# A hybrid decoder layer on one core: the scratch for dynamic transfers goes from 2048 to 4096 bytes, and a 1 KB buffer moves into the 4 KB slots

## The chip, the cores and the metric

The kernel runs on one core of one Trainium2 chip. The metric is device time in microseconds of one execution. Three runs of the kernel before took 745.06, 747.29 and 750.37 us; the median is 747.29 us. A separate execution was profiled; it took 746.93 us, and the profiler saw a span of 745.2 us from its first to its last instruction.

## The reference

One decoder layer over 512 tokens of width 1024, in float32, cut to what matters here:

```python
xn = rms_norm(h, norm_mix)
proj = xn @ w_in                                  # 1024 x 3128
y_r = rwkv7_group(proj[..., :R_COLS], ...)        # 8 heads of 64, a recurrence over the tokens
y_n = nsa_group(proj[..., R_COLS:], ...)          # compressed, selected and window attention
h = h + concat([y_r, y_n]) @ w_out
h = h + (silu(n @ w_gate) * (n @ w_up)) @ w_down  # n = rms_norm(h, norm_ffn); d_ff = 2816
return rms_norm(h, norm_final)
```

In the attention group, keys and values are compressed: windows of 32 tokens, 16 apart, go through a two-layer MLP (`wk1`, `wk2` for the keys, `wv1`, `wv2` for the values) to 31 compressed tokens for each of the two key heads.

## The kernel before

**Arithmetic.** Each float32 operand of a large product is split into a rounded part and a rest (`split`, lines 149 and 151: ACT writes the rounded part, DVE subtracts it for the rest). A product is then three matmuls (`mm3`, lines 168 to 170).

**Stages, by the profiled span.** The input projection is cut into 16 jobs of some 256 columns (to about 205 us). With the jobs are woven the compressed keys (`hidden`, `compressed`) and the triangular solve of the recurrence (`solve`, `solve2`, `solve4`). The recurrence and the attention follow, woven together, to about 380 us; then the output projection and the second norm (to about 412 us), the feed-forward part (to about 600 us), and the down projection (to the end).

**The feed-forward part** is what most of the dynamic transfers belong to. The gate and the up matrix are cut into 11 column blocks, q = 0 to 10, of 256 columns (class `Weights`). Each block is multiplied with seven products in place of eight, in the manner of Strassen and Winograd, for which sums of weight quarters are needed: t1 = gate upper + up upper, t2 = t1 + up lower, t3 = up upper + up lower. A quarter is 512 x 256 floats, 512 KB; it lies in SBUF as 128 partitions by four rows of 1 KB. For all blocks but q = 1 two of the sums are made by transfers: SP loads a quarter plainly (lines 1173 and 1175), and then POOL issues an accumulating transfer of another quarter on top of it (lines 1177 for t1 and 1178 for t3). The lower up quarter (called b22, line 1174) is a plain load by SP. DVE then adds t1 and b22 (line 1184), and the sums are split into operands (lines 1185 to 1195). The even q hold t1, t2 and t3 in three `t4` slots, the odd q in one `L` slot. That is 20 accumulating transfers of 512 KB in 1 KB rows. The down projection has four more (line 1348), of 512 KB each in 2 KB rows.

**The scratch.** For the transfers that POOL issues the program reserves a scratch at the start of every partition of SBUF. Its size is the argument `dynamic_dma_scratch_size` of the program (line 1424). The tiles are laid out behind it.

**Slots.** Tiles with one tag share a fixed number of slots of the largest tile's size: `t4` has four slots of 4 KB, `rp` one of 1 KB, `L` four of 16 KB, `wraw` three of 8 KB. A tile waits for a slot until an older tile of the tag was last read.

**Order.** The kernel is written as one sequence. A planner (`schedule_with_timeline_sim=True`) orders each engine's instructions and hands out slots by going through the sequence with simulated times; `high_priority`, `rank` and `issue_after` in the code push parts of it forward or back. Each engine then runs its list strictly in order: an instruction that waits holds up all behind it on that engine. On DVE, for instance, line 1184 of one block stands ahead of the last splits of the operands that the block before still needs. POOL's list has the transfers as block 4's t3, block 6's t1, block 5's t1, block 5's t3, block 6's t3.

**The compressed keys.** `compressed` (lines 695 to 728) writes three small tiles with the tag `rp`: two copies `rp` (1 KB a partition, one for each key head, line 707) which the PE reads at line 709, and `kc2` (line 714). In the one slot each waits for the last read of the one before. At that time the `t4` slots hold `cm` (the weights and hidden values of the compression, last read at line 709), and then `blk` and `inv` of the solve and `qt2` of the recurrence.

Of the kernel before, what the change touches and what calls it, by code (L numbers as in the profile page):

```python
# [9 lines left out]
F32R = mybir.dt.float32r  # L10
# [36 lines left out]
def hybrid_layer(ctx: ExitStack, tc: tile.TileContext, x, positions, norm_mix, w_in, mu_shift, w0, w2, a0, a2,  # L47
                 g2, k_k, k_a, r_k, lnx_w, lnx_b, pe_k, wk1, bk1, wk2, pe_v, wv1, bv1, wv2, w_out, norm_ffn,
                 w_gate, w_up, w_down, norm_final, out):
    nc = tc.nc  # L50
# [11 lines left out]
    def ps(tag, shape=(128, 512), dtype=F32):  # L62
        return pp.tile(list(shape), dtype, name="ps_" + tag, tag=tag, bufs=PS_BUFS[tag])
# [4 lines left out]
    def st(shape, tag, bufs=1, dtype=F32):  # L68
        return sb.tile(list(shape), dtype, name=tag, tag=tag, bufs=SB_BUFS.get(tag, bufs))
# [168 lines left out]
    def rotate(o, src, tab, scale=1.0):  # L238

        with rank(200):  # L240
            m, tt, n = src.shape[0:3]
            ACT.activation(o, src, AF.Copy, scale=scale)
            ta, tb = (st([128, 8, 16], "rot", 2)[0:m, 0:tt * n].rearrange("p (t n) d -> p t n d", t=tt) for _ in range(2))
            cosv, sinv = (v[:, :, None, :].to_broadcast([m, tt, n, 16]) for v in tab)
            DVE.tensor_mul(ta, o[:, :, :, 0:16], cosv)
            for a in (0, 8):
                DVE.tensor_mul(tb[:, :, :, a:a + 8], o[:, :, :, 8 - a:16 - a], sinv[:, :, :, a:a + 8])
            DVE.tensor_add(o[:, :, :, 0:16], ta, tb)
# [445 lines left out]
    def compressed():  # L694

        p = ps("s")
        for u in range(2):
            PE.matmul(p[0:64, 0:64], hidT[:, 0, u], wc2[:, 0, u], start=u == 0, stop=u == 1)
        kct = st([64, 1, 1, 64], "kct")
        rotate(kct, p[0:64, None, None, 0:64], (rope[0:64, 0, 4:5], rope[0:64, 1, 4:5]))  # L700
        kct = kct[:, 0]
        vcb = st([128, 2, 4, 64], "lora")
        POOL.memset(vcb, 0.0)
        for g in range(2):
            p = ps("s")
            rp = st([128, 2, 4, 32], "rp")
            ACT.activation(rp, hidT[:, 1, :, None, g * 32:g * 32 + 32].to_broadcast([128, 2, 4, 32]), AF.Copy)
            for u in range(2):
                PE.matmul(p[:, 0:64], rp[:, u].rearrange("p a n -> p (a n)"), wc2[:, 1, u], start=u == 0, stop=u == 1)
            for h in range(4):  # L710
                DVE.tensor_copy(vcb[h * 32:h * 32 + 32, g, h], p[h * 32:h * 32 + 32, 0:64])
        kcA = st([128, 2, 2, 32], "kcA", dtype=F32R)
        kc2 = st([64, 4, 64], "rp", dtype=F32R)
        for a in range(2):
            ACT.activation(kc2[:, a], kct[:, 0], AF.Copy)
        for a in range(2):
            DVE.tensor_sub(kc2[:, 2 + a], kct[:, 0], kc2[:, 0].bitcast(F32))
        p = ps("s")
        for a in range(2):
            PE.transpose(p[:, a * 64:a * 64 + 64].bitcast(F32R), kc2[:, 2 * a:2 * a + 2].rearrange("p a d -> p (a d)"), identr[0:64, 0:64])  # L720
        kcA0 = st([128, 64], "rot", 2)
        POOL.memset(kcA0, 0.0)
        ACT.activation(kcA[:, :, 0], p[:, 0:64].rearrange("p (g n) -> p g n", g=2), AF.Copy)
        DVE.tensor_copy(kcA[:, :, 1], kcA0.rearrange("p (g n) -> p g n", g=2))
        for g in range(2):
            gs = slice(g * 64, g * 64 + 64)
            ACT.activation(kcA[gs, g, 1], p[gs, 64 + g * 32:96 + g * 32], AF.Copy)
        T.update(vcb=vcb, kcA=kcA)
# [24 lines left out]

    hk, hv = lambda: hidden(0, "bk1"), lambda: hidden(1, "bv1")
    jobs = [(None, job_lat), (load_tail, job_tail), (cols(1024), job_v(0)), mk[0], then((cols(1280), job_v(1)), gate), mk[1], then((cols(512), job_k(0)), hk), mv[0], (cols(768), job_k(1)), then(mv[1], hv), then((cols(0), job_r(0)), solve, compressed), (cols(256), job_r(1)), then((lambda: load_kv(128), job_vt), solve2), (lambda: load_kv(0), job_ks), then((cols(RCOLS), job_qs(0)), solve3, solve4), (cols(RCOLS + 256), job_qs(1))]

    moving = [jobs[i][1] for i in (3, 5, 7, 9, 12, 13, 14, 15)]
# [677 lines left out]
```

## Time and profile before

| | |
|---|---|
| median of three runs | 747.29 us (745.06 to 750.37) |
| the profiled execution | 746.93 us, span 745.2 us, so 1.73 us outside the span |
| PE busy | 720.3 us, 97% of the span |
| DVE, ACT, POOL busy | 591.9, 402.0, 150.8 us |
| mean granted TensorE clock | 0.983 |
| transfers issued by SP (plain) | 71.91 MB |
| transfers issued by POOL (accumulating) | 12.58 MB |

Busy time is by engine. Matmuls are pipelined and overlap in the records, so a busy PE can still be fed more slowly than it could run; the number of matmuls that start in a stretch tells more. A wait shown as "issue" is time in which the engine waited for nothing that the profile shows. A wait for several things is put down to the one that ended last by the records.

### The profile page before, as it was taken

What the parts mean: (1) busy time and instruction counts of PE and PEld (TensorE: products, weight loads), DVE (VectorE), ACT (ScalarE), POOL (GpSimd) and SP (SyncE); (2) the same over time, 40 slices, a digit from 0 to 9 for tenths busy, and PEclk for the clock granted to TensorE, in tenths of its full rate; (3) what the DMA queues carried; (4) which work ended last, traced back from release to release, by engine and by line L of the source; (5) the groups of instructions that cost most, each with busy time, mean ns of one, the idle gap of its engine ahead of it and who ended that gap; (6) DMA issues with size and microseconds to landing.
All of it is one profiled execution on the core that took longest, in us unless ns stands there. A gap on an engine that the chain in (4) does not pass through costs nothing.

```text
span 745.2 us, 14931 instructions
## 1 busy us (share of the span) xinstructions
PE 720.3 (97%) x6045; PEld 627.3 (84%) x6045; DVE 591.9 (79%) x1097; ACT 402.0 (54%) x670; POOL 150.8 (20%) x250
## 2 busy tenths in 40 slices
PE   6999999998989999999999999989999999999996
PEld 6967887898878788777788999989999999777885
DVE  4488778889767998888368999769796899999835
ACT  6388835325267865778438644444453455465414
POOL 3210030228434552354000001211110101000000
PEclk8999999999899999999999999999999999999998
DMA  7623543100044000140320668787868619352402
GB/s 254 200 88 113 168 115 113 58 2 1 2 144 114 3 2 2 34 138 1 111 88 1 157 188 221 185 181 173 213 166 215 143 63 324 122 118 109 142 0 113
DMA packets 71882, 85.44 MB, mean 115 GB/s; under 512 B 4948, under 2 KB 61350, under 8 KB 71814
## 3 DMA queue, kind: packets, MB, share of 16 engines
q1 hardware_dynamic: 60166, 71.91, 29.4%
q0 software_dynamic: 11648, 12.58, 10.9%
q8 instruction: 47, 0.77, 0.4%
q14 instruction: 21, 0.17, 0.1%
HBM read 82.39 MB, written 2.10 MB: 113 GB/s over the span
## 4 chain that ended last, share of the span: by engine, by line
PE 60%; DVE 22%; DMA 7%; issue 5%; ACT 4%; POOL 1%; SPq 0%; DVEq 0%; POOLq 0%; ACTq 0%
PE ps_ra L169 5%; PE ps_ra L170 5%; PE ps_ra L168 5%; PE ps_pj L170 5%; PE ps_pj L168 5%; PE ps_pj L169 5%; DVE wlo L151 4%; PE ps_o L1019 3%; DVE whi L151 3%; PE ps_pj L1010 2%; DVE L L151 2%; DMA L<-in_w_up_dram 2%; PE ps_s L170 2%; PE ps_s L168 2%; PE ps_s L169 2%
## 5 line engine op out<-in xcount | busy, mean ns | idle before, releaser
L149 ACT ACTIVATE whi<-wraw 128x1024 fp32r<-128x1024 f32 (+1 forms) x63 | 62.6, 1030 | 38.9 <-PE ps_ra L170 13.9
L151 DVE TENSOR_TENSOR wlo<-wraw,whi 128x1024 fp32r<-128x1024 f32 (+1 forms) x46 | 55.2, 1227 | 19.2 <-ACT whi L149 14.3
L1007 POOL TENSOR_SCALAR whi<-whi,m,gates 128x128 f32<-128x128 f32 (+3 forms) x64 | 46.3, 758 | 49.5 <-DVE m L1004 40.1
L170 PE MATMUL ps_ra<-L,wlo 128*128 128x512 f32 (+2 forms) x136 | 47.8, 352 | 0.0
L168 PE MATMUL ps_pj<-L,whi 128*128 128x512 f32 (+1 forms) x128 | 44.3, 351 | 0.5 <-DVE t L1261 0.4
L169 PE MATMUL ps_pj<-L,whi 128*128 128x512 f32 (+1 forms) x128 | 44.7, 349 | 0.0
L169 PE MATMUL ps_ra<-L,whi 128*128 128x512 f32 (+2 forms) x128 | 44.1, 344 | 0.0
L168 PE MATMUL ps_ra<-L,whi 128*128 128x512 f32 (+2 forms) x128 | 43.8, 344 | 0.0
L170 PE MATMUL ps_pj<-L,wlo 128*128 128x512 f32 (+1 forms) x128 | 43.2, 337 | 0.1
L1003 ACT ACTIVATE whi<-whi,m 128x128 f32<-128x128 f32 (+3 forms) x64 | 35.5, 556 | 7.2 <-DVE m L1002 6.8
L168 PE MATMUL ps_ra<-whi,L 128*128 128x256 f32 (+1 forms) x108 | 35.3, 330 | 0.5 <-ACT L L149 0.5
L169 PE MATMUL ps_ra<-wlo,L 128*128 128x256 f32 (+1 forms) x108 | 34.8, 323 | 0.2 <-DVE wlo L151 0.2
L170 PE MATMUL ps_pj<-whi,L 128*128 128x256 f32 (+1 forms) x108 | 34.9, 323 | 0.0
L169 PE MATMUL ps_pj<-wlo,L 128*128 128x256 f32 (+1 forms) x108 | 34.8, 322 | 0.0
L168 PE MATMUL ps_pj<-whi,L 128*128 128x256 f32 (+1 forms) x108 | 34.8, 325 | 0.0
L170 PE MATMUL ps_ra<-whi,L 128*128 128x256 f32 (+1 forms) x108 | 34.5, 322 | 0.0
L1002 DVE CUSTOM_DVE_ANT_0 whi<-ps_s,negb 128x128 f32<-128x128 f32 (+3 forms) x64 | 29.4, 484 | 3.0 <-PE ps_pj L1010 2.0
L170 PEld LDWEIGHTS ps_ra<-L,wlo 128*128 128x128 f32 (+1 forms) x136 | 25.1, 184 | 4.1 <-issue 0.5
L168 PEld LDWEIGHTS ps_pj<-L,whi 128*128 128x128 f32 x128 | 24.0, 188 | 4.3 <-DVE t L1261 0.8
L170 PE MATMUL ps_s<-L,whi 128*128 128x256 f32 (+1 forms) x88 | 26.2, 299 | 1.3 <-DVE whi L151 1.3
L1177 POOL DMA_DIRECT2D t<-in_w_up_dram x6 | 8.0, 1331 | 94.8 <-DVE b L1103 58.5
L170 PEld LDWEIGHTS ps_pj<-L,wlo 128*128 128x128 f32 x128 | 24.0, 188 | 3.5 <-DVE wlo L151 0.9
(708 smaller groups left out, 2546.7 us busy)
## 6 DMA issues: line engine op xcount, KB each, us to landing
wraw<-in_w_gate_dram SPq DMA_DIRECT2D x22, 512.0 KB
wraw<-in_w_in_dram SPq DMA_DIRECT2D x9, 1024.0 KB
wraw<-in_w_down_dram SPq DMA_DIRECT2D x9, 1024.0 KB
t<-in_w_up_dram POOLq DMA_DIRECT2D x12, 512.0 KB, 6.1
wraw<-in_w_up_dram SPq DMA_DIRECT2D x11, 512.0 KB
wraw<-in_w_out_dram SPq DMA_DIRECT2D x4, 1024.0 KB
L<-in_w_up_dram POOLq DMA_DIRECT2D x8, 512.0 KB, 6.8
wraw<-in_w_in_dram SPq DMA_DIRECT2D x6, 512.0 KB
```

Source lines behind the costliest of these rows:

```text
L149: ACT.activation(hi, src, AF.Copy)
L151: (POOL if pool else DVE).tensor_sub(lo, src, hi.bitcast(F32))
L168: PE.matmul(o, lh, rh, start=start, stop=False)
L169: PE.matmul(o, lh, rl, start=False, stop=False)
L170: PE.matmul(o, ll, rh, start=False, stop=stop)
L1002: DVE.tensor_tensor_reduce(pr[:, i], pS[:, i], negb[:, S - n:S], scale=-1.0, scalar=3e38, op0=OP.add, op1=OP.min, accum_out=m[:, i, 0:1])
L1003: ACT.activation(pr[:, i], pr[:, i], AF.Exp, scale=-1.0, bias=m[:, i, 0:1], accum_out=m[:, i, 1:2])
L1007: POOL.tensor_scalar(pr[:, i], pr[:, i], m[:, i, 2:3], gv[:, 1 + b0 + i, h:h + 1], op0=OP.mult, op1=OP.mult)
L1010: PE.transpose(pT[:, j], prr[:, x, j * 128:j * 128 + 128], ident)
L1019: PE.matmul(po[q, 2 * g:2 * g + 2], vtok[:, j % (t + 1), b0 + j // (t + 1), g], pTs[:, par, j], start=False, stop=g == 1 and bs[-1] == 1 a ...
L1177: POOL.dma_start(self.t1, self.quarter(w_up, 0), accum_op=OP.add)
```

## The change

The scratch gets twice its size. It takes 2048 bytes more of each partition. The three tiles of `compressed` get the tag `t4` in place of `rp`: the 1 KB slot of `rp` goes, and the tiles use the 4 KB slots that other tiles share. Nothing else in the source is changed; the planner goes through the changed program anew.

```diff
         for g in range(2):
             p = ps("s")
-            rp = st([128, 2, 4, 32], "rp")
+            rp = st([128, 2, 4, 32], "t4")
             ACT.activation(rp, hidT[:, 1, :, None, ...
...
-        kc2 = st([64, 4, 64], "rp", dtype=F32R)
+        kc2 = st([64, 4, 64], "t4", dtype=F32R)
...
-    nc = _bacc.Bacc("TRN2", ..., num_devices=1, dynamic_dma_scratch_size=2048)
+    nc = _bacc.Bacc("TRN2", ..., num_devices=1, dynamic_dma_scratch_size=4096)
```

## Rows read from the trace of the kernel before

**Rows 1.** The page, part 1: busy us (share of span) x instructions.

```profile
PE 720.3 (97%) x6045; PEld 627.3 (84%) x6045; DVE 591.9 (79%) x1097; ACT 402.0 (54%) x670; POOL 150.8 (20%) x250
```

**Rows 2.** PE's waits, 412 to 600 us: us in total, times, longest.

```profile
PE ps_pj L170 <- DVE wlo L151: 2.4, 1, 2.4
PE ps_ra L170 <- DVE wlo L151: 0.9, 1, 0.9
```

**Rows 3.** DVE's timeline: start, us, line, tiles, [idle before <-releaser].

```profile
497.85 1.23 DVE L1184 TENSOR_TENSOR L<-L,wraw 128x1024 f32<-128x1024 f32 x1 [6.97 <-DMA L<-in_w_up_dram]
499.59 1.22 DVE L151 TENSOR_TENSOR wlo<-wraw,wlo 128x1024 fp32r<-128x1024 f32 x1
...
536.64 1.23 DVE L1184 TENSOR_TENSOR L<-L,wraw 128x1024 f32<-128x1024 f32 x1 [3.77 <-DMA wraw<-in_w_up_dram]
...
577.77 1.23 DVE L1184 TENSOR_TENSOR L<-L,wraw 128x1024 f32<-128x1024 f32 x1 [5.84 <-DMA L<-in_w_up_dram]
```

**Rows 4.** Windows of 5 us: busy us (x starts) by engine, PEclk, DMA share, GB/s.

```profile
490.00:495.00 5.00, 5.00 (x45) 5.00 (x44) 0.88 (x1) 1.06 (x1) 1.30 (x1) 1.00 0.70 206
495.00:500.00 5.00, 3.50 (x31) 3.29 (x29) 2.15 (x3) 0.29 (x1) 1.29 (x1) 1.00 0.56 90
500.00:505.00 5.00, 4.14 (x23) 4.14 (x24) 5.00 (x7) 3.18 (x4) 0.77 (x1) 0.68 1.07 229
```

**Rows 5.** POOL's timeline, 475 to 493 us, columns as in rows 3.

```profile
475.34 1.29 POOL L1178 DMA_DIRECT2D t<-in_w_up_dram  x1 [7.99 <-issue]
481.62 1.29 POOL L1177 DMA_DIRECT2D t<-in_w_up_dram  x1 [4.99 <-DVE whi L151]
491.98 1.30 POOL L1177 DMA_DIRECT2D L<-in_w_up_dram  x1 [9.08 <-issue]
```

**Rows 6.** POOL's waits put down to "issue": us in total, times, longest.

```profile
POOL L L1178 <- issue: 27.4, 4, 8.9
POOL L L1177 <- issue: 9.1, 1, 9.1
```

**Rows 7.** POOL's timeline in the down projection, columns as in rows 3.

```profile
619.28 1.20 POOL L1348 DMA_DIRECT2D wraw<-in_w_down_dram  x1 [33.85 <-DVE wraw L1347]
620.87 1.20 POOL L1348 DMA_DIRECT2D wraw<-in_w_down_dram  x1 [0.39 <-DVE wraw L1347]
```

**Rows 8.** The chain of waits, 436 to 498 us: start, us, what.

```profile
436.78 4.69 DMA wraw<-in_w_up_dram
...
450.29 8.39 DMA t<-in_w_gate_dram
458.75 7.30 issue
...
491.98 5.84 DMA L<-in_w_up_dram
```

**Rows 9.** SP's timeline: block 5's t1 and b22.

```profile
479.78 0.37 SPq L1173 DMA_DIRECT2D L<-in_w_gate_dram  x1
...
488.07 0.37 SPq L1174 DMA_DIRECT2D wraw<-in_w_up_dram  x1
```

**Rows 10.** Line 1177, all its transfers: us from issue to landing.

```profile
DMA to landing us min/median/max: 5.8/7.6/10.1
```

**Rows 11.** Timeline of POOL and DVE around the solve.

```profile
132.84 0.96 POOL L555 MEMSET t<- 128x1024 f32 x1
133.75 1.05 POOL L807 TENSOR_TENSOR t<-b,dend 128x512 f32<-128x512 f32 x1
...
162.49 0.24 POOL L566 TENSOR_TENSOR smask<-t,t 128x31 f32<-128x31 f32 x1
...
197.91 1.30 DVE L577 STREAM_TRANSPOSE t<-L 128x512 f32<-128x512 f32 x2
```

**Rows 12.** PE's timeline at the solve's end, and PE's reads of `rp`.

```profile
205.56 2.21 PE L582 MATMUL ps_s<-t,L 32*32 32x32 f32 x128
...
L709 PE MATMUL ps_s<-t,rp x8: 218/274/275, 160.2 to 163.7; 128*128 128x64 f32 x8
```

More of the change, by code (lines that the diff above doesn't have):

```diff
@@ L1422 @@
     from concourse.bass_utils import run_bass_kernel_spmd as _run
-    nc = _bacc.Bacc("TRN2", target_bir_lowering=False, num_devices=1, dynamic_dma_scratch_size=2048)
+    nc = _bacc.Bacc("TRN2", target_bir_lowering=False, num_devices=1, dynamic_dma_scratch_size=4096)
     arrays, args = {}, []
```

## The prediction

> **What bounds the kernel now.** First the busy times [rows 1]: PE is busy for 720.3 us of the 745.2 us span, so all that faster transfers can give back is time in which PE starves or runs slowly: 24.9 us of idle time in the whole span, plus what it loses at a lower clock. POOL is busy a fifth of the time; what it does matters only where somebody waits for it.
>
> Then PE's waits in the feed-forward part, where 20 of the 24 accumulating transfers are issued [rows 2]. There are only two: 2.4 us and 0.9 us, both for DVE's split of an operand. The windows around the first show its whole cost [rows 4]: 45 matmuls start in the undisturbed 490 to 495 us, but 31 and 23 in the next two windows. In the second of these the mean granted clock is 0.68: it fell from the higher level (2.4 GHz) to the lower (1.2 GHz) for a part of the window, after the pause. 36 matmuls are missing, at 5/45 = 0.111 us each: **4.0 us**, of which 2.4 are the pause and 1.6 the clock.
>
> Then what DVE waited for [rows 3]. It sat idle for 6.97 us ahead of line 1184 (block 5's t1 + b22), until POOL's transfer into t1 had landed, at 497.85 us. The split that PE lacked (line 151, at 499.59) has its input in `wraw` and waits only for its turn behind line 1184. So PE starves when DVE waits longer than about 6.97 - 2.4 = 4.6 us at line 1184. Block 9 shows the same: 5.84 us of wait, 0.9 us of pause, a cover of 4.9 us. Block 7's 3.77 us cost PE nothing.
>
> Last, why t1 was late. On POOL's list the transfer into block 5's t1 left at 491.98, after 9.08 us in which POOL waited for nothing that the profile shows [rows 5]; the four waits of this kind at line 1178 in odd blocks sum to 27.4 us [rows 6], and line 1178 has three more in even blocks. The chain shows such a wait by itself [rows 8]: block 4's t1 had its plain load landed at 458.7, and then 7.30 us passed with no releaser. Two transfers of 1 KB rows never leave less than about 6 us apart (475.34 and 481.62 are the closest in these rows), about as long as the shortest takes to land, 5.8 us [rows 10]. Two of 2 KB rows, with the same bytes and half the rows, leave 1.59 us apart, the second only 0.39 us after POOL was done with the first [rows 7]. I read this as room: 2048 bytes of scratch hold the rows of one 1 KB-row transfer (512 rows), but not of two, and hold two with 256 rows each.
>
> **The change, part by part.**
>
> The scratch. With room for twice the rows, at least two transfers are under way. POOL's eight unexplained waits shrink; seven of them are at lines that nobody waited for long afterwards, and cost nothing now. Line 1178's t3 is used later than t1, and PE's two pauses are both behind a t1. The term is block 5's t1. Its plain load leaves SP at 479.78 [rows 9]. Nearest rows for such a 512 KB load: 4.69 and 8.39 us to land [rows 8]; so t1 is ready for the accumulation between 484.5 and 488.2. The accumulation takes 5.8 to 10.1 us, median 7.6 [rows 10]. Line 1184 could start between 490.3 and 498.3. I take the slow load (four are queued together) and the 5.84 us that this very transfer took: 494.0. With the median it is 495.8. Its other input, b22, leaves SP at 488.07 and by the short row lands at 492.8; that is what is late next, with DVE free from about 490.9. To spare PE the whole pause, line 1184 must start at 497.85 - 2.4 = 495.5. So the pause goes, and the lower clock after it: **-4.0 us**; at the late end (498.3) the gain is nothing. Everything from there to the end is driven by PE's progress and by slots that its progress frees, so the 4.0 us should stay. Block 9's pause stays as well: its t1 is not held back by an older transfer but by its own load, and I count 0 for it (0.9 us if it went).
>
> The issuing. The same 24 transfers are issued, with POOL busy about 1.3 us on each, as before: 0.
>
> The tiles. Two `rp` copies and `kc2` now take three turns in the `t4` slots. The second copy no longer waits for PE's last read of the first: 0, since PE shows no pause there. But a copy now sits in a slot from 139 us until PE has read it at 163.7 [rows 12], while `cm`, `blk`, `inv` and `qt2` want all four. POOL's clearing of `inv` (line 555) and the first write into `qt2` (line 807), now at 132.84 and 133.75, could be pushed behind that read, 0.96 + 1.05 = 2.0 us of work ahead of the solve's first step at 162.49 [rows 11]. The solve would then start up to 163.7 + 2.0 - 162.5 = 3.2 us later. What hides it: DVE's last transposes end at 199.2 [rows 11], and PE turns to what they give at 205.56 [rows 12], 6.3 us later, with projection matmuls in between. Cost 0; without that cover 3.2 us.
>
> The sum: 746.93 - 4.0 = 742.9 us against the profiled execution, which lies 0.36 us under the median of 747.29. Against the median: **743.3 us**.
>
> A rule beside this. The transfer that I let go earlier does so into windows in which the engines that move bytes are busy for 0.70 (490 to 495) and 0.56 of the time (495 to 500) [rows 4]. If the same bytes only change their order, what can be won until 497.85 is the idle share: 0.30 x 5 + 0.44 x 2.85 = 2.75 us. Line 1184 would start at 495.1, still ahead of 495.5. The Trainium skill states this as a rule (page "DMA: Bandwidth & Descriptors", section "Issuing engines are not separate DMA queues"): transfers from all issuers end up on the same 16 engines and interleave, so issuing more at a time saves only issue time. By that rule alone the gain would be near nothing, and it is part of the second rival.
>
> **The rivals.**
>
> 1. *Order shifts to the better or leaves more out.* The planner goes through the changed program anew from line 707 on (139 us), with other slots, and its lists may change anywhere behind. If it also puts block 5's t1 ahead of block 6's, or spares block 9's pause and one pause with a lower clock of the size above, that is -4.0 - 4.0 and some more: 735 to 739.5 us. For it: PE loses 24.9 us in all, most of it outside the feed-forward part. Against: nothing in the profile says which way a new order falls.
>
> 2. *Nothing happens.* Either the landing is no earlier (engines shared, the 498.3 of the late end), or the wait at POOL is not room but one accumulation excluding the next. Against the latter stands the pair at 619.28 and 620.87 [rows 7]. Time 746 to 748.
>
> 3. *Slower: b22 becomes late.* In most blocks b22, which SP loads, is what line 1184 waits for, as in block 7 [rows 3]. Transfers that leave earlier share the engines with it. Where DVE's wait there passes 4.6 us, PE stops, and a pause like block 5's costs 4.0 us. Block 7 needs 0.9 us more for that. Two such pauses, with block 5's kept: 747.3 + 8.0 = 755.3 us. It decides when b22 lands more than about a microsecond later in two blocks. Against: block 7's is the longest wait of this kind now, and t3 stands behind t1 on POOL's list, so what is let go earlier is mostly what comes after.
>
> **How the numbers follow.** Forecast 0.52 (741 to 745.5), rival 1 0.18, rival 2 0.18, rival 3 0.12. Of the runs, 1% is about what a measurement of this kernel can tell from no change: 739.8 to 754.8. Faster by more than that is rival 1: 0.18. Slower is most of rival 3: 0.10. The rest, 0.72, is within 1%. The range of 737 to 753 leaves out a third of rival 1 and most of rival 3, about 0.15.
>
> **What would show it.** Right: POOL's "issue" waits at lines 1177 and 1178 nearly gone; pairs of transfers leaving some 1.5 us apart; DVE's wait at line 1184 of block 5 under 4.6 us, then for b22; no window near 0.68 of the clock in the feed-forward part, which is about 4 us shorter; the solve's end no later for PE. Wrong: transfers still 6 us apart (no room gained); t1 landing at the same distance behind its plain load (rival 2); PE pauses at other blocks with DVE waiting for b22 (rival 3); or the difference lying ahead of 400 us, where only a new order can have made it.

## The result: 0.5% slower, and the profile after

The changed kernel takes 751.37 us (median of 21 runs, 746.92 to 753.94) against 747.52 us of the kernel before, run beside it on the same chips. The ratio is 1.0053, 95% interval 1.0039 to 1.0068: 3.9 us slower, small but clear. The forecast was 743.3 us. The profiled execution took 751.61 us, its span is 749.9 us.

The page of the changed kernel, part 1, answers [rows 1]:

```profile
PE 724.0 (97%) x6045; PEld 629.6 (84%) x6045; DVE 593.3 (79%) x1097; ACT 403.0 (54%) x670; POOL 150.9 (20%) x250
```

Busy times say little: PE is busy 3.7 us longer with the same 6045 matmuls. So the two traces are laid side by side by landmarks, instructions that both have once in the same role: the first matmul of line 588 (second half of the solve's end), the first of line 826 (first step of the recurrence), the first of line 1108 (feed-forward part begins), and POOL's first transfer of line 1348 (early in the down projection, when the first buffers are free for it). One execution of each kernel, in us from the span's start:

| kernel | L588 | L826 | L1108 | L1348 | L1108 to L1348 |
|---|---|---|---|---|---|
| before | 210.4 | 223.8 | 398.6 | 619.3 | 220.7 |
| after | 218.6 | 233.4 | 408.6 | 623.3 | 214.7 |

Two effects of opposite sign: 9.6 us are lost before the recurrence begins, and 6.0 us are won in the feed-forward part.

**The gain** is where the forecast had it. PE's waits from 412 to 600 us in the changed kernel (us in total, times, longest) answer [rows 2]; no split of an operand is left among them:

```profile
PE ps_s L168 <- ACT wlo L149: 0.4, 1, 0.4
PE ps_s L1108 <- DVE b L1097: 0.3, 1, 0.3
PE ps_s L1108 <- ACT L L1110: 0.3, 1, 0.3
```

POOL's timeline of the changed kernel around blocks 4 to 6 answers [rows 5], with start, us, line, tiles and [idle before <-releaser]. Transfers of 1 KB rows now leave 1.17 us apart (458.71, 459.88), where it was 6.1 us at best, and none waits with "issue" as its releaser [rows 6]:

```profile
458.71 1.29 POOL L1177 DMA_DIRECT2D L<-in_w_up_dram  x1 [17.42 <-DVE t L1258]
459.88 1.41 POOL L1178 DMA_DIRECT2D L<-in_w_up_dram  x1
...
496.12 1.28 POOL L1177 DMA_DIRECT2D L<-in_w_up_dram  x1 [9.95 <-DVE t L1265]
498.48 1.28 POOL L1178 DMA_DIRECT2D L<-in_w_up_dram  x1 [1.08 <-DMA L<-in_w_up_dram]
```

DVE's line 1184 of block 5 answers [rows 3]: its wait fell from 6.97 to 3.54 us, under the 4.6 us of cover, and it is now b22 (`wraw`) that came last:

```profile
504.21 1.23 DVE L1184 TENSOR_TENSOR L<-L,wraw 128x1024 f32<-128x1024 f32 x1 [3.54 <-DMA wraw<-in_w_up_dram]
```

The windows of 5 us around it answer [rows 4]. 45 or 46 matmuls start in each, at the full clock; before, it was 31 and 23 in the two windows of the pause:

```profile
495.00:500.00 5.00, 5.00 (x46) 5.00 (x46) 4.11 (x5) 3.13 (x4) 2.56 (x2) 1.00 0.60 136
500.00:505.00 5.00, 5.00 (x45) 5.00 (x45) 1.46 (x2) 1.06 (x1) 0.00 (x0) 1.00 1.15 266
505.00:510.00 5.00, 5.00 (x46) 5.00 (x46) 5.00 (x7) 3.60 (x4) 1.23 (x1) 1.00 0.91 196
```

**The loss** begins with the slots. In the changed kernel the planner gives two of the four t4 slots to the two `rp` copies at once, which ACT writes at 160.9 and 161.2 us (before: 139.3 and 160.9). `inv` and `qt2` come after them. POOL's timeline of the changed kernel answers [rows 11]:

```profile
163.66 0.15 POOL L722 MEMSET rot<- 128x64 f32 x1 [30.54 <-DVE kct L248]
164.82 0.95 POOL L555 MEMSET t<- 128x1024 f32 x1 [1.01 <-ACT t L715]
165.74 1.05 POOL L807 TENSOR_TENSOR t<-b,dend 128x512 f32<-128x512 f32 x1
...
166.97 0.24 POOL L566 TENSOR_TENSOR smask<-t,t 128x31 f32<-128x31 f32 x1
```

The clearing of `inv` went from 132.84 to 164.82 us, and the solve's first step from 162.49 to 166.97: 4.5 us. That is still less than the 6.3 us of cover. But the cover itself had moved. The planner laid PE's, DVE's, ACT's and POOL's lists anew between about 139 and 225 us, presumably because the solve now ends later in its simulation; SP's list and POOL's order of transfers stayed as they were. DVE's timeline, first one line of the kernel before, then the changed one, shows what stands ahead of the solve's transposes (lines 573 and 577) now:

```profile
200.35 0.42 DVE L538 TENSOR_TENSOR L<-ps_o,amask 128x256 f32<-128x256 f32 x1 [1.13 <-PE ps_o L532]
```

```profile
205.89 0.42 DVE L538 TENSOR_TENSOR L<-ps_o,amask 128x256 f32<-128x256 f32 x1 [5.52 <-PE ps_o L532]
206.23 0.68 DVE L806 TENSOR_TENSOR b<-b,dend 128x512 f32<-128x512 f32 x1
206.83 2.27 DVE L573 STREAM_TRANSPOSE L<-t 128x1024 f32<-128x1024 f32 x1
209.14 1.30 DVE L577 STREAM_TRANSPOSE t<-L 128x512 f32<-128x512 f32 x2
```

Line 577 started at 197.91 before [rows 11], 11.2 us earlier; L538 (ps_o) stood behind it. PE's L582, which needs it, answers [rows 12]; it started at 205.56 before, 8.1 us earlier:

```profile
213.66 2.21 PE L582 MATMUL ps_s<-t,L 32*32 32x32 f32 x128
```

Line 538 waits for PE, whose list is what matters. Two things in it differ. Line 532 (small products, 64 x 64) alternates with single projection matmuls (lines 168 to 170) 14 times in place of 11. And of the projection matmuls that remain after that, 47 stand ahead of L582, 18 between L582 and L588, and none behind; it was 26, 22 and 17. PE's and the other engines' windows, first of the kernel before, then of the changed one (PE, PEld, DVE, ACT, POOL busy us (x starts), PEclk, DMA share, GB/s):

```profile
195.00:200.00 5.00, 5.00 (x23) 3.21 (x24) 4.06 (x6) 0.00 (x0) 1.26 (x5) 0.80 0.00 0
200.00:205.00 5.00, 5.00 (x25) 4.88 (x26) 1.12 (x3) 0.60 (x1) 0.00 (x0) 0.52 0.01 3
205.00:210.00 5.00, 5.00 (x154) 4.83 (x153) 0.76 (x4) 2.36 (x4) 0.00 (x0) 1.00 0.01 3
```

```profile
190.00:195.00 5.00, 4.45 (x59) 3.58 (x61) 4.97 (x17) 1.26 (x2) 4.22 (x11) 0.87 0.00 0
195.00:200.00 5.00, 5.00 (x24) 3.29 (x25) 3.48 (x13) 0.00 (x0) 3.06 (x12) 0.50 0.00 0
200.00:205.00 5.00, 5.00 (x18) 3.17 (x18) 0.34 (x2) 0.00 (x0) 0.00 (x0) 0.50 0.00 0
205.00:210.00 5.00, 5.00 (x22) 4.66 (x23) 4.07 (x5) 0.18 (x1) 0.79 (x2) 0.50 0.01 3
210.00:215.00 5.00, 5.00 (x113) 4.87 (x114) 1.30 (x5) 0.51 (x2) 0.00 (x1) 0.92 0.00 0
225.00:230.00 5.00, 2.68 (x18) 2.52 (x18) 4.04 (x8) 1.94 (x5) 1.55 (x2) 0.50 1.00 356
```

PE is "busy" in both, but in the changed kernel it runs at 0.50 of the clock (1.2 GHz) from 195 to 210 us, in the kernel before only for a part of 195 to 200 and most of 200 to 205. One alternation takes 0.57 us at the full clock and 0.91 us at half of it, as two stretches of PE's timeline show, the kernel before (194.85 to 195.42) and the changed one (198.48 to 199.39):

```profile
194.85 0.38 PE L170 MATMUL ps_pj<-whi,L 128*128 128x256 f32 x1
195.17 0.32 PE L532 MATMUL ps_o<-L,b 64*64 64x64 f32 x2
195.42 0.38 PE L168 MATMUL ps_pj<-whi,L 128*128 128x256 f32 x1
```

```profile
198.48 0.58 PE L170 MATMUL ps_pj<-whi,L 128*128 128x256 f32 x1
198.99 0.47 PE L532 MATMUL ps_o<-L,b 64*64 64x64 f32 x2
199.39 0.58 PE L168 MATMUL ps_pj<-whi,L 128*128 128x256 f32 x1
```

The second thing shows in PE's waits of the changed kernel, 186 to 236 us. Behind L588 no projection matmul is left to run while DVE copies (line 590) and masks (line 800); the kernel before waits 0.7 us at L811, and 1.0 us at L948 for POOL. First its lines, then those of the changed kernel:

```profile
PE ps_s L948 <- POOL wlo L945: 1.0, 2, 0.7
PE ps_ra L811 <- DVE whi L800: 0.7, 1, 0.7
```

```profile
PE ps_s L948 <- DVE L L590: 2.4, 2, 1.5
PE ps_ra L811 <- DVE whi L800: 2.3, 1, 2.3
PE ps_s L532 <- DVE L L538: 1.1, 1, 1.1
```

From the first L532 to the first L826 the kernel before takes 36.5 us (187.3 to 223.8) and the changed one 46.8 (186.6 to 233.4): 10.3 us more. The first L588 to the first L826 takes 13.4 and 14.8 us, but before 17 matmuls of 0.118 us (2.0 us) stand in it and now none, so the bare chain went from 11.4 to 14.8: 3.4 us. Not all of that is waiting: behind the pauses the clock fell once more (0.50 from 225 to 230 us, in the windows above), while the kernel before had 1.00 from 205 us to L826. The other 6.9 us lie ahead of L588.

### The profile page after: what moved, and what is told of

The parts are those of the page before. It is cut to its first block, busy times and chain, and to the rows that moved or that the text cites. A ratio compares the mean times of both kernels' runs of the same rounds, so it can differ in the third digit from the quotient of the medians.

```text
span 749.9 us, 14933 instructions
## 1 busy us (share of the span) xinstructions
PE 724.0 (97%) x6045; PEld 629.6 (84%) x6045; DVE 593.3 (79%) x1097; ACT 403.0 (54%) x670; POOL 150.9 (20%) x250
## 4 chain that ended last, share of the span: by engine, by line
PE 71%; DVE 18%; ACT 3%; DMA 3%; issue 2%; POOL 0%; SPq 0%; DVEq 0%; ACTq 0%; POOLq 0%
PE ps_pj L170 7%; PE ps_pj L168 6%; PE ps_pj L169 6%; PE ps_ra L169 6%; PE ps_ra L168 6%; PE ps_ra L170 6%; PE ps_s L168 3%; PE ps_s L169 3%; PE ps_s L170 3%; PE ps_o L1019 3%; DVE wlo L151 3%; PE ps_pj L1010 2%; DVE L L151 2%; DMA L<-in_x_dram 1%; DVE whi L151 1%
## 5 line engine op out<-in xcount | busy, mean ns | idle before, releaser
L170 PE MATMUL ps_pj<-whi,L 128*128 128x256 f32 (+1 forms) x108 | 35.9, 333 | 0.2 <-DVE L L151 0.2
L168 PE MATMUL ps_pj<-whi,L 128*128 128x256 f32 (+1 forms) x108 | 35.7, 333 | 0.0
L168 PEld LDWEIGHTS ps_pj<-L,whi 128*128 128x128 f32 x128 | 24.2, 189 | 3.6 <-ACT whi L149 0.6
L169 PEld LDWEIGHTS ps_pj<-L,whi 128*128 128x128 f32 x128 | 24.3, 190 | 3.4 <-DVE L L151 0.4
```

Of the source, the lines that this page charges most:

```text
L168: PE.matmul(o, lh, rh, start=start, stop=False)
L169: PE.matmul(o, lh, rl, start=False, stop=False)
L170: PE.matmul(o, ll, rh, start=False, stop=stop)
```

## The experiments

Twelve kernels were run. All lists named below are the engines' instruction lists in order; "alternations" and "projection matmuls ahead of L582 / between / behind L588" are counted on PE's. Ratios are against the kernel before, run beside each on the same chip; they are not quotients of the medians shown, since different kernels ran on different chips.

| kernel | scratch, bytes | alternations | ahead / between / behind | median, us | ratio, 95% interval | first L532 to L826 | L1108 to L1348 |
|---|---|---|---|---|---|---|---|
| before | 2048 | 11 | 26 / 22 / 17 | 747.5 | 1 | 36.5 | 220.7 |
| after | 4096 | 14 | 47 / 18 / 0 | 751.4 | 1.0053 (1.0039 to 1.0068) | 46.8 | 214.7 |
| s3072 | 3072 | 11 | 26 / 22 / 17 | 744.8 | 0.9967 (0.9948 to 0.9986) | 37.8 | 217.9 |
| t4_2048 | 2048 | 14 | 47 / 18 / 0 | 753.4 | 1.0077 (1.0047 to 1.0107) | 46.8 | 219.6 |
| s2560 | 2560 | 11 | 26 / 22 / 17 | 745.5 | 0.9987 (0.9968 to 1.0005) | 36.7 | 218.9 |
| g1t4_3072 | 3072 | 9 | 20 / 22 / 23 | 744.5 | 0.9966 (0.9947 to 0.9984) | 38.0 | 216.5 |
| s3584 | 3584 | 11 | 26 / 22 / 17 | 744.9 | 0.9984 (0.9967 to 1.0001) | 36.6 | 218.7 |
| v3_0 | 4096 | 0 | 79 / 6 / 0 | 753.0 | 1.0094 (1.0072 to 1.0116) | 37.3 | 219.2 |
| v3_110 | 4096 | 33 | 23 / 22 / 10 | 769.7 | 1.0318 (1.0290 to 1.0346) | 55.0 | 217.2 |
| t2_4096 | 4096 | 11 | 43 / 22 / 0 | 757.7 | 1.0151 (1.0129 to 1.0174) | 41.5 | 218.3 |
| t3odd_3584 | 3584 | 11 | 26 / 22 / 17 | 751.1 | 1.0071 (1.0044 to 1.0098) | 39.4 | 222.0 |
| rp_3072 | 3072 | 14 | 47 / 18 / 0 | 750.7 | 1.0074 (1.0048 to 1.0100) | 42.1 | 217.3 |
| t2_smask_t4 | 4096 | 7 | 23 / 22 / 20 | 743.8 | 0.9967 (0.9952 to 0.9982) | 36.2 | 217.4 |
| smask_t2_t4 | 4096 | 13 | 12 / 22 / 31 | 749.0 | 1.0044 (1.0021 to 1.0068) | 42.2 | 215.9 |

The last two columns are from one execution each, and they vary: from L532 to L826 36.5 to 39.4 us with PE's list of the kernel before, 42.1 to 46.8 us with that of the changed kernel. The medians decide on the total, the columns only where it lies. Some of the profiled executions lie off their kernel's median: s3072 and v3_0 2.6 us and smask_t2_t4 3.1 us above it, v3_110 3.1 us below.

**s3072: the scratch without the move.**

```diff
-dynamic_dma_scratch_size=2048
+dynamic_dma_scratch_size=3072
```

> Scratch of 3072 bytes, the three tiles keep their own slot `rp`; all engines have the instruction order of the kernel before. Theory A (the loss of 9.9 us ahead of 231 us comes from the order that the move into the t4 slots leads to, the gain of 5.5 us from the scratch alone): 747.5 - 5.5 = 742 us (741 to 743.5), PE's matmul L582 at about 205.6 us as before, no PE pause of 2.4 us before 505 us, POOL's waits without a releaser at lines 1177 and 1178 nearly gone. Rival B (the larger scratch costs the early time, through other tile addresses or more transfers at a time): 752 us or more, with L582 near 213 us. Third possibility: 3072 bytes are no room for a second transfer of 512 rows: 747.5 us, transfers still 6 us apart.

744.8 us, 2.5 us faster (1.0 to 3.9). All lists are those of the kernel before, and L532 to L826 takes 37.8 us, not 46.8: the size of the scratch does not make the early loss, and rival B falls. The gain is real but smaller than 5.5 us. The trace shows what took the rest: PE's waits, 412 to 600 us, in s3072:

```profile
PE ps_s L170 <- DVE wlo L151: 1.1, 1, 1.1
PE ps_pj L170 <- DVE wlo L151: 0.6, 1, 0.6
```

DVE's line 1184 of blocks 5 and 7 in s3072 says why: both wait longer than 4.6 us for t1. Block 7's had waited 3.77 us for b22 before and cost nothing [rows 3].

```profile
499.30 1.23 DVE L1184 TENSOR_TENSOR L<-L,wraw 128x1024 f32<-128x1024 f32 x1 [5.98 <-DMA L<-in_w_up_dram]
...
539.58 1.23 DVE L1184 TENSOR_TENSOR L<-L,wraw 128x1024 f32<-128x1024 f32 x1 [6.50 <-DMA L<-in_w_up_dram]
```

The pauses were 0.6 and 1.1 us, so the cover was 5.4 us here, more than the 4.6 us read from the kernel before. Block 5's t1 left at 491.68 and landed 7.6 us later, in place of 5.84 [rows 8]; block 7's took 9.6 us. That they share the engines with more transfers now is the likely reason; t3odd_3584 below bears on it.

**t4_2048: the move without the scratch.**

```diff
-rp = st([128, 2, 4, 32], "rp")
+rp = st([128, 2, 4, 32], "t4")
...
-kc2 = st([64, 4, 64], "rp", dtype=F32R)
+kc2 = st([64, 4, 64], "t4", dtype=F32R)
```

> The three tiles in the t4 slots, scratch of 2048 bytes as before; all engines have the instruction order of the changed kernel. Theory A: 747.5 + 9.9 = 757.4 us, or somewhat less if later stages hide some of it (754 to 758.5); L582 near 213.7 us; in the feed-forward part the 2.4 us pause as before. Rival B: 747.5 us (746 to 749), L582 near 205.6 us.

753.4 us, 5.8 us slower (3.5 to 8.0), a little under the expected range's lower end. The 10.3 us ahead of L826 are all there, and so is the pause of the feed-forward part (2.1 us). The move makes the loss, alone. How large it is differs between executions of these same lists: the one with the highest mean granted clock (0.985) took 747.8 us, the six others (0.972 to 0.981) 751.6 to 754.9.

**s2560: how much room two transfers need.**

```diff
-dynamic_dma_scratch_size=2048
+dynamic_dma_scratch_size=2560
```

> Scratch of 2560 bytes, everything else and all orders as before. If two transfers of 512 rows need only little more than the 2048 bytes: the whole gain, 742 us, transfers 1.2 to 2.4 us apart. If room goes in proportion to the rows, as the prediction read it (2048 bytes for 512 rows, so 4096 for two): 747.5 us, transfers 6 us apart. Between: a gain at some transfers only, 743 to 747 us.

745.5 us; the interval (0.9968 to 1.0005) just includes no change. But the transfers are plain to see. POOL's timeline of s2560, block 5:

```profile
490.69 1.30 POOL L1177 DMA_DIRECT2D L<-in_w_up_dram  x1 [11.51 <-DVE b L1267]
491.79 1.51 POOL L1178 DMA_DIRECT2D L<-in_w_up_dram  x1
498.45 1.28 POOL L1178 DMA_DIRECT2D t<-in_w_up_dram  x1 [5.15 <-issue]
```

512 bytes more are enough for a second transfer of 512 rows, 1.1 us behind the first; the third waits as before. So room is not in proportion to the rows.

**g1t4_3072: one copy in a t4 slot.**

```diff
-rp = st([128, 2, 4, 32], "rp")
+rp = st([128, 2, 4, 32], ("rp", "t4")[g])
...
-dynamic_dma_scratch_size=2048
+dynamic_dma_scratch_size=3072
```

> Scratch of 3072 bytes; of the three tiles only the second copy `rp` sits in a t4 slot. POOL's clearing of inv (L555) then stands early again, the first write into qt2 (L807) behind the solve's start, and DVE's transposes L573 and L577 ahead of the last product L538 of the inner part, as in the kernel before. Theory A in the form 'two slots taken at once push the solve back': early loss under 3 us, 741 to 745 us, L582 at 205 to 208 us. If any copy in a t4 slot costs the whole: 752 us, L582 near 213 us. If 3072 bytes are no room for two transfers, 5.5 us more in each case.

744.5 us, as s3072. With one slot taken `inv` is cleared early again (132.2 us), `qt2` is written late (164.3), and nothing is lost. It takes both copies at once.

**s3584: room for a third transfer.**

```diff
-dynamic_dma_scratch_size=2048
+dynamic_dma_scratch_size=3584
```

> Scratch of 3584 bytes, the three tiles keep the slot `rp`; orders as before. With 3072 bytes the third transfer of a group still waited 4.5 to 7.3 us at POOL, with 4096 it did not. If room for a third transfer is worth something: 741.5 to 743.5 us, a further 1 to 3 us under the 744.8 of 3072 bytes, and no wait without a releaser at line 1178. If only the second transfer matters: 744.8 us again (743.5 to 746).

744.9 us: no further gain. The waits with "issue" at line 1178 are gone, and still PE pauses 1.8, 0.5 and 0.4 us behind a late split. The third transfer was not what mattered.

**v3_0 and v3_110: two other lists for PE.** Both are the changed kernel with one rank changed.

```diff
-        with rank(-100):
+        with rank(0):         # v3_0
+        with rank(-110):      # v3_110
             rb = T["rb"]
             inner(1)
```

> The changed kernel with the rank of `solve3` at 0 in place of -100. On PE's list the pairs of small products (L532) then alternate with single projection matmuls 2 times in place of 14; 79 projection matmuls stand ahead of L582, 6 between L582 and L588 and none behind (47, 18 and none in the changed kernel). Theory (a): the early loss is mostly the slow alternation at the low clock, 5.5 us: 746 us or less (744 to 748), with L532 done before 200 us and no long stretch at a clock of 0.5 there. Theory (b): it is mostly the cover that is missing behind L588 (PE pauses at L948 and L811): 751 to 755 us, with pauses there as long or longer.

> The changed kernel with the rank of `solve3` at -110 in place of -100. On PE's list the small products alternate with single matmuls about 45 times in place of 14; 23 projection matmuls stand ahead of L582, 22 between L582 and L588, 10 behind. POOL's clearing of inv is as late as in the changed kernel. Theory (a): 31 more alternations at 0.3 to 0.45 us: 759 us or more. Theory (b): cover as in the kernel before, 745 to 748 us, without the pauses at L811 of 2.3 us.

The lists have 0 and 33 alternations, not the 2 and 45 written down. Both kernels clear `inv` as late as the changed one (163.7 and 162.8 us). v3_0 needs 37.3 us from the first L532 to L826, though PE pauses 2.2 us at L948 and 1.4 us at L811, and v3_110 needs 55.0: so the late clearing decides nothing by itself, PE's list does, and alternations cost as theory (a) says. The total of v3_0 missed, 753.0 in place of 746 us: the rank also changed the lists of the recurrence, where 10.8 us are lost between L826 and L1108 (222.2 to 407.8, against 174.8 us before). So its total tests nothing.

**t2_4096: alternations as before, cover gone.**

```diff
-rp = st([128, 2, 4, 32], "t4")
+rp = st([128, 2, 4, 32], "t2")
...
-kc2 = st([64, 4, 64], "t4", dtype=F32R)
+kc2 = st([64, 4, 64], "t2", dtype=F32R)
```

> Scratch of 4096 bytes, the three tiles in the t2 slots in place of t4, so that inv and qt2 are not pushed back. On PE's list 11 alternations as in the kernel before, but 43 projection matmuls ahead of L582, 22 between and none behind L588. Theory (a): no early loss, L588 at about 212 us, 742 to 744 us. Theory (b): pauses at L948 and L811 as in the changed kernel, some 4 us: 746 to 748 us. If the late clearing of inv by itself makes the loss: 742 us as well, but with pauses that cost nothing.

`inv` is cleared early (133.8 us) and the solve's first step comes at 159.0, ahead of the kernel before, yet 5.0 us are lost up to L826, with PE's pauses of 2.2 us at L948 and 2.3 us at L811. So the missing cover costs by itself, without slots and without a late solve: theory (b) has a part. The total, 757.7 us, is again mostly lost in the recurrence (181.6 us from L826 to L1108).

**t3odd_3584: t1 alone on the engines.**

```diff
-                POOL.dma_start(self.t3, self.quarter(w_up, 1), accum_op=OP.add)
+                if self.q % 2 == 0: POOL.dma_start(self.t3, self.quarter(w_up, 1), accum_op=OP.add)
...
                 DVE.tensor_add(self.t2, self.t1, self.b22)
+                self.q % 2 and self.q > 1 and (DVE.scalar_tensor_tensor(self.t3[0:1, 0, 0:8],
+                    self.t2[0:1, 0, 0:8], 0.0, self.t3[0:1, 0, 0:8], op0=OP.mult, op1=OP.add),
+                    POOL.dma_start(self.t3, self.quarter(w_up, 1), accum_op=OP.add))
...
-dynamic_dma_scratch_size=2048
+dynamic_dma_scratch_size=3584
```

> Scratch of 3584 bytes, `rp` kept, PE's and DVE's orders as in the kernel before; in the odd blocks the accumulating transfer into t3 is held back until line 1184 has read t1 (a small DVE instruction that reads t2 and writes eight elements of t3 unchanged). With 2560 to 3584 bytes t3 left 1.1 to 2.2 us behind t1, and t1 landed 7.5 to 9.6 us after its issue, where it had taken 5.84 us alone. Theory S (the two share the engines, and that gave back part of the 4.0 us): t1 lands 5.8 to 6.5 us after its issue, line 1184 of block 5 starts some 5 us earlier than in the kernel before in relation to the blocks around it, no PE pause over 0.5 us between 412 and 600 us; 741 to 743.5 us. Rival: t1 is slowed by the plain loads of b22 and t3 anyway: it lands after 7.5 us or more, pauses of 1 to 2 us stay, 744 to 745.5 us.

751.1 us, 0.87% slower than s3584 by the two ratios, and theory S falls: without t3 behind it, block 5's t1 left at 495.54, line 1184 could start only 8.4 us later (503.90), and the pause of 2.4 us was back. The rival's reading stands: SP's plain loads run beside it (b22 left at 494.70, the next block's t3 at 495.80). In the kernel before, t1 left 3.9 us behind b22 [rows 5, 9] and had the engines more to itself. The hold also changed POOL's and DVE's lists from about 453 us on, so the total has more in it than the one transfer.

**rp_3072: the copies without `kc2`.**

```diff
-rp = st([128, 2, 4, 32], "rp")
+rp = st([128, 2, 4, 32], "t4")
...
-dynamic_dma_scratch_size=2048
+dynamic_dma_scratch_size=3072
```

> Scratch of 3072 bytes; only the two `rp` copies in the t4 slots, `kc2` keeps the 1 KB slot. The lists at the solve are those of the changed kernel (47 projection matmuls ahead of L582, 14 alternations). If the two copies make the loss and kc2 nothing: 750 to 752 us, with PE at the low clock from about 194 to 210 us and the first L826 at about 232 us. If kc2 has a part in it: 745 to 749 us.

750.7 us (ratio 1.0074): the two copies make the loss, `kc2` has no part that shows.

**t2_smask_t4 and smask_t2_t4: the whole change with other slots.** Scratch 4096, no slot `rp`, and behind the solve all lists as before.

```diff
-rp = st([128, 2, 4, 32], "t4")
+rp = st([128, 2, 4, 32], ("t2", "smask")[g])   # t2_smask_t4
+rp = st([128, 2, 4, 32], ("smask", "t2")[g])   # smask_t2_t4
```

> Scratch of 4096 bytes and no slot `rp`, as in the changed kernel; the first copy in a t2 slot, the second in the slot smask, `kc2` in t4. Behind 230 us all lists are those of the kernel before. On PE's list: 7 alternations of small products and single matmuls (14 in the changed kernel, 11 before), 23 projection matmuls ahead of L582, 22 between L582 and L588, 20 behind (47, 18, 0 and 26, 22, 17). If the order of PE's list makes the whole early loss, whatever the reason for it: first L826 at 222 to 226 us, the gain in the feed-forward part kept (220.7 us between the first L1108 and the first L1348 before, 214.7 after the change): 739 to 743 us. If the scratch of 4096 bytes or the missing slot has a cost of its own: 748 us or more.

> As t2_smask_t4 with the two copies' slots exchanged. On PE's list 13 alternations, nearly as many as in the changed kernel, but 12 projection matmuls ahead of L582, 22 between L582 and L588, 31 behind. Theory (a), the alternation at the low clock is the larger part of the early loss: the small products are done at 203 to 206 us, first L826 3 to 6 us later than before, 745 to 748 us. Theory (b), the missing cover behind L588 is the larger part: first L826 within 2 us of before, 740 to 743 us, without the pauses at L948 and L811.

t2_smask_t4 takes 743.8 us, 2.5 us less than the kernel before (1.3 to 3.6) and 6.4 us less than the change as it was made (0.86% by the two ratios), by one line. It beats both kernels; s3072 and g1t4_3072 do so by the same margin. `inv` is cleared at 161.5 us, nearly as late as in the changed kernel, and the first L826 comes at 224.8.

smask_t2_t4 takes 749.0 us, just above theory (a)'s range. Its windows show the low clock with 13 alternations:

```profile
200.00:205.00 5.00, 5.00 (x19) 3.19 (x19) 2.88 (x4) 0.00 (x0) 0.79 (x2) 0.59 0.00 0
205.00:210.00 5.00, 5.00 (x38) 4.09 (x39) 1.02 (x2) 0.00 (x0) 0.00 (x0) 0.50 0.01 3
210.00:215.00 5.00, 5.00 (x127) 4.94 (x122) 0.00 (x0) 2.84 (x5) 0.00 (x0) 0.50 0.01 3
```

Its cover behind L588 is whole, and PE's waits show it, 186 to 236 us: 0.5 us at L811 in place of 2.3, and nothing behind line 590:

```profile
PE ps_s L948 <- POOL wlo L945: 1.2, 2, 0.9
PE ps_ra L811 <- DVE whi L800: 0.5, 1, 0.5
```

Still 5.7 us are lost from the first L532 to L826 (42.2 against 36.5). Another 4.0 us lie ahead of the first L532; PE waited 4.5 us for lines 711 and 634 there, where the kernel before waits 2.2 for line 634, and the rest of the 4.0 is open. This execution is one of the longer ones of its kernel: of the twelve, the four with a mean granted clock of 0.976 or less took 751.3 to 754.3 us, the eight others (0.978 to 0.989) 746.0 to 751.2.

What each theory is worth can be read at L588, with the projection matmuls behind it taken out at 0.118 us each. Behind L588 the kernels with no such matmul left lose 3.4 us (the changed kernel), 3.3 (t4_2048), 3.9 (rp_3072), 4.6 (t2_4096) and 1.6 (v3_0) against the kernel before, and smask_t2_t4, with 31 of them, 0.4. That is the missing cover, theory (b), with the low clock that follows its pauses. Ahead of L588 the changed kernel and t4_2048 lose 6.9 and 7.0 us, and smask_t2_t4 5.2, but rp_3072 only 1.6, and it has the changed kernel's 14 alternations in the same order. Its windows from 195 to 210 us show what differs, the clock:

```profile
195.00:200.00 5.00, 5.00 (x25) 3.28 (x25) 3.51 (x12) 0.00 (x0) 3.40 (x13) 0.91 0.00 0
200.00:205.00 5.00, 5.00 (x21) 4.04 (x21) 2.50 (x3) 0.00 (x0) 0.00 (x0) 0.50 0.01 3
205.00:210.00 5.00, 5.00 (x63) 4.87 (x64) 2.74 (x7) 0.60 (x1) 0.79 (x2) 0.91 0.00 0
```

So the alternations cost much when the clock falls early among them, and little when it does not; what decides that in one execution is open. Both theories have a part; the sizes are from single executions.

## Why the prediction was wrong, step by step

**The room: right.** 2048 bytes held one transfer of 512 rows at a time: each of the eight unexplained waits ended 0.3 us after the transfer before had landed (block 5's t1 left at 491.98, the one before landed at 491.67). Every larger scratch let the second go 1.1 to 2.4 us behind the first. Only the proportion was wrong: 2560 bytes do for two.

**The term of -4.0 us: right in place, too large by the whole times.** In the six kernels with 4096 bytes the lists are those of the kernel before from 5 us behind L1108 on, by line, operation and tile. From L1108 to L1348 they are shorter than its 220.7 us by 6.0 (after), 4.8 (smask_t2_t4), 3.5 (v3_110), 3.3 (t2_smask_t4), 2.4 (t2_4096) and 1.5 us (v3_0), 3.6 on the mean; t4_2048, with the old scratch, is shorter by 1.1, so a part of this is the spread of single executions. By whole times the scratch is worth less: 2.5 us in s3072, 1.0 and 1.2 in s2560 and s3584 with intervals that reach no change, and 1.8 between t4_2048 and the changed kernel, which have equal lists throughout. Line 1184 of block 5 waited 3.5 to 4.3 us in five of the six, under the 4.6 us that the prediction set as its limit, and 5.9 in v3_0. In the changed kernel b22 came last, as it said, in the five others t1. Block 9's 0.9 us, counted at 0, went to 0.4 or less. What the term left out is the other blocks: with 2560 to 3584 bytes t1's wait is 3.9 to 7.2 us at blocks 5, 7 and 9, pauses of 0.4 to 1.8 us stay or appear there, and the part is 1.8 to 4.2 us shorter. That 4096 bytes do better than 3584 is not shown; no run here has 4096 bytes with all the lists of the kernel before.

**The rule of the shared engines**, named beside the sum, holds in one half. Block 5's t1 landed in 5.84 us when it left 2.8 us behind the last plain load, and in 6.2 to 9.0 us in the thirteen other kernels, where a plain load left at most 1.3 us before it or shortly after it. The Trainium skill (page "DMA: Bandwidth & Descriptors", section "Issuing engines are not separate DMA queues") says that transfers started by any engine run on the same 16 engines and interleave, and the traces agree. The Trainium skill's other half there, that starting transfers on several engines at once saves only the time of issuing, does not cover this case. Here a wait for room held back what stood behind on one engine's list, POOL's, and ending it was worth 2.5 us (s3072).

**The tiles at 0: the step that failed.** The prediction saw the push: `inv` and `qt2` behind PE's read of the copies, the solve up to 3.2 us later; it was 4.5. It then set this against 6.3 us of cover and wrote "Cost 0; without that cover 3.2 us". That judged a new slot by the old lists. The planner went through the program anew and laid the cover elsewhere; why it chose these lists no run shows. PE turned to the transposes' result at 213.66, 8.1 us later, where the prediction had it no later at all. Measured, the step costs 5.8 us (t4_2048, 3.5 to 8.0), and even its upper bound of 3.2 us was too low, since it priced a delay and not an order. The delay alone costs little: v3_0 and t2_smask_t4 clear `inv` late as well (163.7 and 161.5 us) and take 37.3 and 36.2 us from L532 to L826, against 36.5. The two parts run alone add up: 5.8 us for the move and -2.5 for the scratch (s3072) give 3.3, and 3.9 were measured. The prediction's last sign of being wrong, a difference ahead of 400 us that only a new order can have made, is the one that came.

**The issuing at 0** held: SP's list and POOL's order of transfers are unchanged, and POOL's busy time is 150.9 us after 150.8.

**The rivals.** Rival 1 named the mechanism that decided, a new order from line 707 on, but priced it only to the better; the sentence that nothing in the profile says which way a new order falls was a reason to price both. Rival 2 is refuted: transfers leave 1.17 us apart, and s3072 is clearly faster. Rival 3, b22 late and PE paused twice more, did not come. A relative of it did: block 7's line 1184, bounded by b22 before, waited 6.5 us for t1 in s3072, 7.2 in s3584 and 6.4 in t2_smask_t4, and PE paused 1.0 to 1.8 us.

## What to carry to other kernels

A tile moved into a shared pool of slots is priced in two steps: what it pushes back, and then what the planner's lists become when it knows of that; here the push cost little and the new lists 5.8 us, and only the new lists show that. So compare the engines' instruction lists before trusting a cover taken from the old trace. And where a change has two parts, ask whether each needs the other: here 512 bytes more of scratch let the second transfer go (a clear gain in time took 1024 bytes more, s3072), and other slots for the two copies kept a gain of 2.5 us.

## What was not expected of the hardware

PE's clock fell while PE showed no idle time. In the kernel before, PE is busy without a gap from 185 to 205 us, and yet at 198.0 us, in the midst of the alternation with 64-column products, it went to the lower level (1.2 GHz): matmuls of 256 columns that followed each other at 0.118 us did so at 0.213. In the changed kernel it fell at 193.5 us, after a pause of 1.1 us that ended at 190.55. In both it rose again when only projection matmuls ran (204.7 and 210.6 us). How much of such a stretch falls to the low level differs between executions that have this part of PE's list in common: in the changed kernel, t4_2048 and rp_3072 L532 to L826 took 46.8, 46.8 and 42.1 us, with a granted clock of 0.50, 0.50 and 0.91 from 195 to 200 us.

An accumulating transfer occupies the engines that move bytes for longer than a plain load of the same size. Two windows of the kernel before, the first with mostly block 5's accumulation, the second with plain loads only, about half of their packets of 2 KB and more: 0.87 of the engines' time for 145 GB/s against 0.98 for 344. In the first, 473 packets of the accumulation, of about 1 KB, took 80.6% of the engines' time, and 100 packets of plain loads, also of about 1 KB, 6.8%: about 2.5 times as long for one.

```profile
493.00:497.00 4.00, 4.00 (x38) 4.00 (x37) 0.00 (x0) 0.00 (x0) 0.28 (x1) 1.00 0.87 145
221.00:224.00 3.00, 1.84 (x19) 1.42 (x19) 2.06 (x3) 2.91 (x7) 1.43 (x3) 1.00 0.98 344
```
